# Out-projection of six feature blocks as fill of the scan's last chain, the first feed-forward pair in column halves, and an even spread of the modulation sums

## The chip, the cores and the metric

One core of a Trainium2 chip runs the whole kernel. The metric is the device time of one execution in microseconds, the median of several runs. TensorE (PE), VectorE (DVE), ScalarE (ACT), GpSimd (POOL) and SyncE (SP) each work through their own list of instructions in order; SP, and in places ACT and POOL, also issue the transfers (DMAs).

## What is computed

Two layers act on 512 tokens of 1,024 features, with 256 context tokens. The part that matters here is the first layer: an rwkv7 mixer (a scan in two directions over 16 heads), its out-projection, and a dense gated feed-forward.

```python
s_kk = einsum('bhvk,bhk->bhv', s, kk_t)          # one step of the scan
s = s * w_t - s_kk * (kk_t * a_t) + v_t * k_t
y_t = einsum('bhvk,bhk->bhv', s, r_t)
...
yn = ((y - mean) * rsqrt(var + 64e-5)) * lnx_g + lnx_b     # per head
mix = ((yn + coef * v) * gate) @ w_o                       # out-projection, 1024 x 1024
x = layer_norm(ALPHA * x + ada_gate * mix)                 # ALPHA = 4 ** 0.25
h = x * (1 + ada_scale) + ada_shift
x = layer_norm(ALPHA * x + ada_gate2 * ((silu(h @ w1) * (h @ w3)) @ w2))   # inner size 2816
```

The scales, shifts and gates ("modulations") are products of a conditioning vector with matrices of 1024 x 6144. Two more modulation vectors, called "1" and "2", are needed by the layers that follow.

## The kernel before

Every product of two float32 matrices is made from parts: each operand is split into a high part (an ACT cast to fp32r, `L167`) and a low part (a DVE subtraction, `L168`), and `mm3` issues three matmuls, high by high, high by low and low by high (`L173`).

**The scan** (`phase_rwkv`). The features are cut into 8 blocks f of 128. Each block has a chain of 12 steps; a step is a row of short dependent instructions: the ACT copy `Rs` (`L863`), PE matmuls (`L833`), the ACT copy `UV` (`L871`), PE again, and the DVE state update `S` (`L888`, `L890`). Between the links of the chain the program puts other work by `fill(n)`. It draws the next items of the generator `background()`, which holds the jobs of the next blocks' inputs (`job`, its matmuls are `L979`) and then the modulation items "0" (`ada`, matmuls `L235`). How many items are drawn by a slot is read from the table `PACE`; there are 384 slots, 48 to a chain. In `PACE` the last 40 items, all of them modulation items, lie evenly over the slots 268 to 384. The scan matmuls, the jobs and the modulation items share PE's one list. When a chain ends, `tail(f)` normalises its block on DVE, POOL and ACT, adds the bonus, gates it and stores the 128 x 512 block `yn` to `ygd` in DRAM.

**Out-projection and layer norm** (`L2112` to `L2134`). After the last tail the eight blocks are loaded into `xres`, split into the parts `y3`, and then `xres` is loaded anew with x. `w_o` comes as four loads of 1 MB and is split into 8 pairs of parts. For each block of 128 tokens (tb) PE does two halves of 24 matmuls of 128 x 512, `resid_add` adds gate times result (`L1314`, `L1318`), and `norm_tail` does the layer norm: statistics on DVE (`L1130`), the reciprocal root on POOL, the scaling on ACT (`L1139`), the affine part on POOL; at once eight PE transposes (`L1162`) and their splits give the columns of the features `hT`.

**Feed-forward** (`phase_ffn`). 22 inner blocks of 128 in three chunks of 8, 8 and 6. Each inner block (an `out`) takes 48 matmuls of 128 x 512 from `w1` and `w3`, then silu and a split; after each of the first two chunks `down` adds the chunk's product with `w2` (192 matmuls). All of `hT` has to be there before the first matmul. Beside it run the modulation sums (`ada_sum`), a generator `side` of 32 items: 12 groups for "1" and 12 for "2", with the sums of a group (PE, `L274`) three items behind it. A group is 8 loads of 256 KB into three buffers (`L283`) and 8 multiply-adds: on DVE for "1" (`L288`), on ACT and POOL for "2" (`L285`, `L286`). The loads of both are issued by SP, between those of the weights. In the program each `out` draws items: one at the first and two at the second of a pair for the first 16 blocks, then one each. The gates of the sums are read back by POOL (`L301`).

## Time and profile before

| | us |
|---|---|
| median of 3 runs (3021.52 to 3031.95) | 3023.82 |
| the profiled execution, its own time | 3030.04 |
| its span in the trace | 3028.3 |
| TensorE busy in the span | 2658.0 |
| VectorE busy | 1716.0 |
| ScalarE busy | 1333.8 |
| GpSimd busy | 825.0 |

The profiled execution is 6.2 us, or 0.2%, above the median. A busy share tells little by itself, since the stages have different limits; the rows below go by stage. A line of waits reads "engine, what it does, line <- who released it: us in total, times, longest". A line of the timeline gives start, duration, instruction, and in brackets the engine's idle time ahead of it with its releaser. Lines of `L...` are those of the kernel before.

### The profile page before, as it was taken

To read this page: it belongs to the slowest core of one execution; us is meant where nothing else is said; L and a number is where in the kernel's file an instruction comes from. 1 tells how busy PE (TensorE), PEld (TensorE's weight loads), DVE (VectorE), ACT (ScalarE), POOL (GpSimd) and SP (SyncE) were. 2 spreads that over 40 slices of the span, in tenths; PEclk is the share of its full clock that TensorE was granted. 3 is DMA by queue.
4 is the path that set the end of the run, shared out by engine and by line. 5 is a ranking of instruction groups with operands and counts; after the bars stand their busy time and mean duration, and the time that the engine had idled before them with its cause. 6 is when DMAs were issued, how large, how long until landed. Compare 5 with 4: busy or idle time off the path is not lost. (4 is left out here: it accounts for less than half of the span.)

```text
span 3028.3 us, 47973 instructions
## 1 busy us (share of the span) xinstructions
PE 2658.0 (88%) x18816; PEld 2001.1 (66%) x18816; DVE 1716.0 (57%) x2526; ACT 1333.8 (44%) x2338; POOL 825.0 (27%) x908
## 2 busy tenths in 40 slices
...
GB/s 257 182 222 66 96 125 142 181 137 129 172 133 95 186 129 165 222 189 212 186 150 63 306 258 271 258 258 287 233 239 88 68 43 74 56 84 94 102 90 64
DMA packets 301823, 477.92 MB, mean 158 GB/s; under 512 B 47282, under 2 KB 176067, under 8 KB 294935
## 3 DMA queue, kind: packets, MB, share of 16 engines
...
## 5 line engine op out<-in xcount | busy, mean ns | idle before, releaser
L168 DVE TENSOR_TENSOR wl<-w,wh 128x1024 fp32r<-128x1024 f32 (+2 forms) x400 | 477.3, 1203 | 622.3 <-ACT wh L167 618.9
L167 ACT CAST wh<-w 128x1024 fp32r<-128x1024 f32 (+2 forms) x400 | 382.8, 966 | 636.4 <-PE mm L173 438.8
L173 PE MATMUL mm<-act,wh 128*128 128x512 f32 x1408 | 441.1, 395 | 18.6 <-ACT act L167 14.8
L173 PEld LDWEIGHTS mm<-act,wh 128*128 128x128 f32 x1408 | 266.8, 190 | 78.7 <-ACT act L167 15.4
L173 PE MATMUL mm<-wh,act 128*128 128x512 f32 x948 | 308.1, 402 | 7.8 <-ACT wh L167 4.5
L173 PE MATMUL mm<-act,wl 128*128 128x512 f32 x704 | 277.3, 394 | 4.5 <-DVE wl L168 4.5
L173 PEld LDWEIGHTS mm<-wh,act 128*128 128x128 f32 x948 | 182.4, 194 | 57.3 <-issue 7.8
L173 PE MATMUL mm<-wl,act 128*128 128x512 f32 x474 | 190.9, 403 | 0.1
L286 POOL TENSOR_TENSOR act<-act 128x512 f32<-128x512 f32 x96 | 145.3, 1513 | 152.8 <-ACT act L285 137.8
L301 POOL DMA_DIRECT2D bc<-gate x6 | 3.6, 592 | 619.2 <-DVEq L1730 516.3
L173 PEld LDWEIGHTS mm<-act,wl 128*128 128x128 f32 x704 | 133.6, 190 | 36.3 <-DVE wl L168 8.4
L799 DVE STREAM_TRANSPOSE XT<-T 128x512 f16<-128x512 f16 x120 | 84.6, 705 | 99.8 <-ACT T L797 99.7
L743 POOL TENSOR_TENSOR GA<-GA,masks 128x512 f32<-128x512 f32 (+1 forms) x96 | 100.2, 1053 | 102.8 <-ACT GA L742 99.6
L285 ACT ACTIVATE act<-act,cT 128x512 f32<-128x512 f32 x96 | 68.4, 724 | 118.4 <-DMA act<-in_w_ada_dram 117.7
L739 PE MATMUL gm<-kr,bk 64*128 64x128 f32 (+1 forms) x768 | 115.7, 327 | 3.8 <-ACT GA L742 2.0
L792 DVE TENSOR_TENSOR W<-pW,masks 128x512 f16<-128x512 f32 x120 | 81.8, 681 | 63.5 <-PE pW L790 59.7
L739 PEld LDWEIGHTS gm<-kr,bk 64*128 64x128 f32 x768 | 99.7, 226 | 24.5 <-ACT GA L742 9.3
L173 PE MATMUL mm<-wh,moxl 128*128 128x512 f32 (+1 forms) x336 | 113.9, 382 | 0.0
L173 PEld LDWEIGHTS mm<-wl,act 128*128 128x128 f32 x474 | 91.8, 194 | 31.1 <-DVE wl L168 5.0
L850 POOL TENSOR_TENSOR SP<-S,pc 128x64 f32<-128x64 f32 x176 | 58.3, 349 | 196.2 <-DVE S L890 184.8
L173 PE MATMUL mm<-wh,moxh 128*128 128x512 f32 (+1 forms) x336 | 107.3, 389 | 4.9 <-ACT wh L167 4.9
L797 ACT CAST T<-pT 128x512 f16<-128x512 f32 x120 | 69.6, 580 | 84.1 <-PE pT L795 80.9
...
## 6 DMA issues: line engine op xcount, KB each, us to landing
w<-in_moe_w_dram SPq DMA_DIRECT2D x136, 512.0 KB
w<-in_moe_w_dram SPq DMA_DIRECT2D x40, 1024.0 KB
w<-in_ffn_w_dram SPq DMA_DIRECT2D x32, 1024.0 KB
...
w<-in_w_up_dram SPq DMA_DIRECT2D x22, 1024.0 KB
x<-xdk POOLq DMA_DIRECT2D x18, 1024.0 KB, 5.7
```

The source lines that it names most:

```text
L167: self.nc.scalar.copy(out=hi, in_=x)
L168: self.nc.vector.tensor_tensor(out=lo, in0=x, in1=hi.bitcast(F32), op=OP.subtract)
L173: self.nc.tensor.matmul(ps, x, y, start=start and i == 0, stop=stop and i == 2, skip_group_check=True)
L285: nc.scalar.activation(out=wt, in_=wt, func=AF.Copy, scale=c)
L286: nc.gpsimd.tensor_tensor(out=acc, in0=wt, in1=acc if kk else bias, op=OP.add)
L301: (eng or self.nc.gpsimd).dma_start(out=t, in_=row_ap.to_broadcast([128, D]))
L739: nc.tensor.matmul(pss[par][:, s2, d, :nc_], bkj(d, par, j), KR[d][PR(par), j::12, :][:, :nc_ // 64, :], start=True, stop=True)
L743: nc.gpsimd.tensor_tensor(out=out, in0=out, in1=gm, op=OP.mult)
L792: nc.vector.tensor_tensor(out=W16, in0=pW, in1=lmask[:, li, None].to_broadcast(sh), op=OP.mult)
L797: nc.scalar.copy(out=T16, in_=pT)
L799: nc.vector.transpose(fl(XT), fl(T16))
L850: nc.gpsimd.tensor_tensor(out=SP[:, d], in0=S[:, d], in1=PC[d][:, j:j + 1].to_broadcast([128, 64]), op=OP.mult)
```

## The change

1. `PACE`: the 40 modulation items now end at slot 322, and 50 draws follow up to slot 384, the end of the last chain. They are four jobs "o", one for each 256 output features: the product of feature blocks 0 to 5 with `w_o`, 72 matmuls of 128 x 256 in each (288 in all). Each loads `w_o` twice by SP, and x three times (1 MB each) by POOL's queue. Its result is gated, added to ALPHA x on DVE and stored to `ysums`.
2. `tail` splits `yn` into its two parts itself and stores them to `yparts`, in place of the store to `ygd`. In the last tail three operations go from POOL to DVE.
3. After the scan only blocks 6 and 7 are projected: 12 matmuls for each tb, where there were 48. Their parts come in two loads of 512 KB by POOL's queue, `xres` is loaded from `ysums`, and `w_o` in one load of 1 MB. The transposes of a tb (`turn`) are put behind the norm of the next one.
4. The first `out` does its columns 0 to 255 first, then `turn(3)`, then columns 256 to 511.
5. The loads of "1" and all bias loads go from SP's queue to POOL's. An item of `side` now follows each `out` and, in the first two chunks, each pair of additions of `down`; it is tied by `issue_after` to the instructions just ahead of it.

```diff
-        (220, 137), (236, 153), (252, 161), (268, 177), (384, 217))
+        (220, 137), (236, 153), (252, 161), (268, 177), (322, 217), (384, 267))
...
-            nc.sync.dma_start(out=bias[0:1], in_=b[None, c0:c0 + n])
+            nc.gpsimd.dma_start(out=bias[0:1], in_=b[None, c0:c0 + n])
             for kk in range(8):
                 wt, c = ws[kk % 3], self.cT[:, kk, row:row + 1]
-                nc.sync.dma_start(out=wt, in_=w[kk * 128:(kk + 1) * 128, c0:c0 + n])
+                (nc.sync if on_pool else nc.gpsimd).dma_start(out=wt, in_=w[kk * 128:(kk + 1) * 128, c0:c0 + n])
...
+    def o_out(p, pss, lat, pool, tag, *_):
+        g = k.t(pool, [128, 512], tag=tag)[:, :256]
+        nc.sync.dma_start(out=g, in_=k.gates["0"][0][:, p * 256:(p + 1) * 256].to_broadcast([128, 256]))
+        for i, ps in enumerate(pss):
+            t = k.t(pool, [128, 512], tag=tag)
+            rows = lambda x: x[i * 256:(i + 1) * 256, p * 256:(p + 1) * 256].rearrange("(b p) n -> p b n", p=128)
+            nc.sync.dma_start(out=halves(t), in_=rows(a["x"][0]))
+            nc.vector.tensor_tensor(out=halves(ps), in0=halves(ps), in1=g[:, None, :].to_broadcast([128, 2, 256]), op=OP.mult)
+            nc.vector.scalar_tensor_tensor(out=t, in0=t, scalar=ALPHA, in1=ps, op0=OP.mult, op1=OP.add)
+            nc.sync.dma_start(out=rows(yo["sums"]), in_=halves(t))
+        return
+    OUT = {"k": k_out, "r": r_out, "v": v_out, "o": o_out}
...
+            eng = nc.gpsimd if f < 7 else nc.vector
...
-            nc.sync.dma_start(out=yg[f], in_=yn)
+            hi, lo = (k.t(bst, [128, 512], F32R, tag="st") for _ in range(2))
+            k.part_to(hi, lo, yn)
+            for i, x in enumerate((hi, lo)):
+                nc.sync.dma_start(out=yo["parts"][:, f, i], in_=x.bitcast(F32))
+            made["y", f] = True
...
+            byrow, last_ = n_ in "vo", (6 if n_ == "o" else KB) - 1
...
+            for kk in range(last_ + 1):
...
+            for p in range(4):
+                assert all(made.get(("y", f)) for f in range(6))
+                yield from job("o", p, True)
...
-def norm_tail(k, sp, psp, tb, xres, gbc, bbc, hT, scol, bcol):
+def norm_rows(k, sp, tb, xres, gbc, bbc):
...
-    if hT is not None:
-        to_feature(k, sp, psp, xh, hT, slice(tb * 128, (tb + 1) * 128), scol, bcol)
+    return xh
...
+        if cols is not None and i == 0:
+            ws = [k.part(w[:, :, :128]) for w in (w1, w3)]
+            pss = [k.t(psp, [128, 512], tag="mm") for _ in ws]
+            for cs, make in cols:
+                make()
+                for w, ps in zip(ws, pss):
+                    for kk in range(KB):
+                        k.mm3(ps[:, cs], at(w, ALL, kk), at(xT, ALL, kk, cs), kk == 0 and cs.start == 0, kk == KB - 1 and cs.stop == n)
+        for w in (w1, w3) if not pss else ():
...
+    done = [0]
+    def tick(n, *behind):
+        with ExitStack() as es:
+            for x in behind:
+                es.enter_context(tc.issue_after(x.ins))
+            for _ in range(n):
+                done[0] += 1
+                if done[0] % 2 == 0:
+                    next(side, None)
...
-                k.part_to(*g[f - f0 + i], s)
-                for _ in range(1 + i if f < 16 else 1):
-                    next(side, None)
+                hi, lo = k.part_to(*g[f - f0 + i], s)
+                tick(2, hi, lo)
...
+        def add(tb, hf, ps):
+            x = resid_add(k, sp, tb, hf, ps, gate2, xres, ALPHA if f0 == 0 else None)
+            if f0 < 16:
+                tick(1, x)
...
-            with tc.tile_pool(reuse_waits="tile", name="wo3", bufs=5) as wo3:
-                y3 = feat()
-                yg = xres.rearrange("p t d -> p (t d)").rearrange("p (f n) -> p f n", f=KB)
-                for f in range(KB):
-                    nc.sync.dma_start(out=yg[:, f, :], in_=ygd[f])
-                for f in range(KB):
-                    k.part_to(*at(y3, ALL, f), yg[:, f, :])
-                nc.sync.dma_start(out=xres, in_=a["x"][0].rearrange("(t p) d -> p t d", p=128))
-                ws = []
-                for i in range(4):
-                    raw = k.load_w(a["rk_w_o"][0][(i % 2) * 512:(i % 2 + 1) * 512, (i // 2) * 512:(i // 2 + 1) * 512])
-                    ws += [k.part(raw[:, 2 * q:2 * q + 2, :], wo3 if len(ws) + q < 5 else k.wq) for q in range(2)]
-                hT = None
-                for tb in range(4):
-                    for hf in range(2):
-                        ps = k.t(psp, [128, 512], tag="mm")
-                        for kk in range(KB):
-                            k.mm3(ps, at(y3, ALL, kk, slice(tb * 128, (tb + 1) * 128)), at(ws[hf * 4 + kk // 2], ALL, kk % 2), kk == 0, kk == KB - 1)
-                        resid_add(k, sp, tb, hf, ps, gate, xres)
-                    hT = hT or feat()
-                    norm_tail(k, sp, psp, tb, xres, *gb, hT, *cols)
+            raw = k.load_w(a["rk_w_o"][0][768:1024, :])
+            ws = [k.part(raw[:, :, hf * 512:(hf + 1) * 512]) for hf in range(2)]
+            y67 = k.t(act, [128, 2, 2, NT], F32R, tag="act")
+            for i in range(2):
+                nc.gpsimd.dma_start(out=y67[:, i], in_=yo["parts"][:, 6 + i])
+            nc.sync.dma_start(out=xres, in_=yo["sums"].rearrange("(t p) d -> p t d", p=128))
+            hT = feat()
+            rows_ = {}
+            def norm(tb):
+                cs = slice(tb * 128, (tb + 1) * 128)
+                for hf in range(2):
+                    ps = k.t(psp, [128, 512], tag="mm")
+                    for i in range(2):
+                        k.mm3(ps, at((y67[:, i, 0], y67[:, i, 1]), ALL, cs), at(ws[hf], ALL, i), i == 0, i == 1)
+                    resid_add(k, sp, tb, hf, ps, gate, xres, None)
+                rows_[tb] = norm_rows(k, sp, tb, xres, *gb)
+            def turn(tb):
+                to_feature(k, sp, psp, rows_[tb], hT, slice(tb * 128, (tb + 1) * 128), *cols)
+            for tb in range(4):
+                norm(tb)
+                if tb:
+                    turn(tb - 1)
+            turns = [(slice(0, 256), lambda: None), (slice(256, 512), lambda: turn(3))]
```

ACT at the end of the scan, last steps of the last chain, before: `Rs` and `UV` belong to the chain, `wh<-w` is the high part of a weight, here always of `w_o` for the stage behind the scan.

```order
L871 ACTIVATE UV_12696<-ch_13601 64x128 x2
L167 CAST wh_13828<-w_13822 128x1024
L167 CAST wh_13834<-w_13832 128x1024
L167 CAST wh_13838<-w_13832 128x1024
L863 COPY Rs_13659<-ch_13646 128x128
L167 CAST wh_13804<-w_13802 128x1024
L167 CAST wh_13808<-w_13802 128x1024
L167 CAST wh_13814<-w_13812 128x1024
L167 CAST wh_13818<-w_13812 128x1024
L167 CAST wh_13824<-w_13822 128x1024
L871 ACTIVATE UV_12696<-ch_13646 64x128 x2
```

The same place after.

```order
L167 CAST wh_14034<-w_14032 128x512
L167 CAST wh_14247<-w_14245 128x1024
L167 CAST wh_14251<-w_14245 128x1024
L877 COPY Rs_14001<-ch_13988 128x128
L885 ACTIVATE UV_12952<-ch_13988 64x128 x2
L167 CAST wh_14494<-w_14490 128x1024
L877 COPY Rs_14062<-ch_14049 128x128
L885 ACTIVATE UV_12952<-ch_14049 64x128 x2
L877 COPY Rs_14115<-ch_14102 128x128
L1373 DMA plb<-in_cpool_dram 128x512
L1375 DMA plw<-in_pool_w_dram 128x8x256
L885 ACTIVATE UV_12952<-ch_14102 64x128 x2
```

Eight casts of `w_o` stood about the last `Rs`; now a cast of an "o" job and two of `w_o` stand ahead of the third last `Rs`, one of the feed-forward's `w1` (`w_14490`) behind the next `UV`, and none between the last two `UV`.

SP from the end of the last tail on, before: `ygd` holds the blocks, `in_ada_w` is the matrix of "1".

```order
L2118 DMA xres<-ygd 128x512 x2
L945 DMA ygd<-yn_13680 128x512
L2118 DMA xres<-ygd 128x512 x6
L2121 DMA xres<-in_x_dram 128x4x1024
L283 DMA act_14236<-in_ada_w_dram 128x512 x3
L280 DMA act_14236<-in_ada_b_dram 1x512
L155 DMA w_14625<-in_ffn_w_dram 128x8x256
L283 DMA act_14236<-in_ada_w_dram 128x512
```

The same place after: `st` are tiles of the "o" jobs and the parts of `yn`, `ysums` and `yparts` the new DRAM tensors.

```order
L371 DMA st_14117<-gate_221 128x256
L155 DMA w_14731<-in_ffn_w_dram 128x8x256
L375 DMA st_14119<-in_x_dram 128x2x256
L375 DMA st_14124<-in_x_dram 128x2x256
L378 DMA ysums<-st_14119 128x2x256
L378 DMA ysums<-st_14124 128x2x256
L963 DMA yparts<-st_14181 128x512
L2164 DMA xres<-ysums 128x4x1024
L963 DMA yparts<-st_14182 128x512
L155 DMA w_14899<-in_ffn_w_dram 128x8x256
```

The load of `xres` stood behind the loads of `ygd`; now it stands behind the last stores of `ysums` and the store of the first part of the last `yn`. The loads of `in_ada_w` have left this engine.

POOL from the end of the layer norm on, before: `bc<-gate` reads a gate of the sums back, `L286` adds up "2".

```order
L1148 TENSOR_TENSOR xres<-rsq_14185,bg_13763 128x1024
L1149 TENSOR_TENSOR xres<-xres,bb_13765 128x1024
L301 DMA bg_16922<-in_ln_g_dram 128x1024
L301 DMA bb_16924<-in_ln_b_dram 128x1024
L301 DMA bc_16917<-gate_14310 128x1024
L286 TENSOR_TENSOR act_14236<-act_14236 128x512 x16
L301 DMA bc_17521<-gate_14311 128x1024
L286 TENSOR_TENSOR act_14236<-act_14236 128x512 x80
```

The same engine in the feed-forward after, from the read of the first gate on.

```order
L301 DMA bc_17237<-gate_14630 128x1024
L283 DMA act_14484<-in_ada_w_dram 128x512 x8
L280 DMA act_14484<-in_ada_b_dram 1x16x32
L283 DMA act_14484<-in_ada_w_dram 128x512 x8
L280 DMA act_14484<-in_ada_b_dram 1x16x32
L283 DMA act_14484<-in_ada_w_dram 128x512 x8
L280 DMA act_14484<-in_ada_b_dram 1x16x32
L283 DMA act_14484<-in_ada_w_dram 128x512 x8
L280 DMA act_14484<-in_b_ada_dram 1x16x32
L283 DMA act_14484<-in_ada_w_dram 128x512 x4
L301 DMA bc_17841<-gate_14631 128x1024
L286 TENSOR_TENSOR act_14484<-act_14484 128x512 x2
```

The loads of "1" now stand on POOL, the last of them behind the read of the first gate of "1" (`gate_14630`), and the first addition of "2" behind the read of the second (`gate_14631`).

## Rows read from the trace of the kernel before

**Rows 1.** Page, its first line.

```profile
span 3028.3 us, 47973 instructions
```

**Rows 2.** Windows: length, busy us of PE, PEld, DVE, ACT, POOL; PEclk, DMA share, GB/s.

```profile
993.30:1052.80 59.50, 48.68 (x926) 33.45 (x927) 30.43 (x65) 26.43 (x69) 22.73 (x49) 0.88 0.59 188
1052.80:1067.00 14.20, 1.44 (x24) 1.06 (x20) 7.70 (x8) 8.47 (x11) 0.00 (x0) 0.50 0.48 165
1067.00:1081.40 14.40, 5.85 (x22) 3.01 (x21) 4.65 (x8) 3.45 (x7) 4.92 (x5) 0.50 0.96 305
...
1100.90:1180.00 79.10, 43.30 (x176) 35.44 (x176) 38.33 (x66) 18.81 (x31) 26.44 (x24) 0.76 0.25 79
...
1195.40:1280.00 84.60, 84.44 (x386) 68.40 (x384) 54.93 (x76) 21.77 (x29) 0.53 (x1) 1.00 0.71 231
1280.00:1305.00 25.00, 4.32 (x18) 4.17 (x19) 17.68 (x28) 3.61 (x5) 0.00 (x0) 0.59 0.52 167
...
1345.00:1577.00 232.00, 223.37 (x985) 177.20 (x983) 111.77 (x103) 121.71 (x169) 145.83 (x97) 0.99 0.60 191
```

**Rows 3.** Waits of PE from 1052 to 1182 us.

```profile
PE mm L1162 <- ACT rsq L1139: 31.3, 4, 12.1
...
PE ch L833 <- ACT Rs L863: 8.4, 1, 8.4
```

**Rows 4.** Timeline of ACT, the last chain's end.

```profile
1059.53 1.99 ACT L167 CAST wh<-w 128x1024 fp32r<-128x1024 f32 x2 [3.71 <-DMA w<-in_rk_w_o_dram]
```

**Rows 5.** Windows of the job matmuls (L979) alone, last thirds of two chains: PE, PEld.

```profile
757.30:795.90 38.60, 14.05 (x57) 8.36 (x57) 1.00 0.56 178
...
967.30:993.30 26.00, 0.00 (x0) 0.00 (x0) 1.00 0.33 95
```

**Rows 6.** Timeline of PE, a run of job matmuls.

```profile
803.12 0.28 PE L979 MATMUL bg<-wl,x 128*128 128x256 f32 x1
...
803.24 0.39 PE L979 MATMUL bg<-wh,x 128*128 128x256 f32 x2
...
803.59 0.28 PE L979 MATMUL bg<-wh,x 128*128 128x256 f32 x1
```

**Rows 7.** Windows of the modulation matmuls (L235) alone, last chain: PE, PEld.

```profile
993.30:1052.80 59.50, 9.79 (x104) 2.25 (x104) 0.88 0.59 188
```

**Rows 8.** Timeline, from the last block's store to the first residual sum.

```profile
1085.15 1.29 DVE L168 TENSOR_TENSOR act<-xres,act 128x512 fp32r<-128x512 f32 x2 [3.78 <-DMA ygd<-yn]
...
1091.65 0.38 SPq L2121 DMA_DIRECT2D xres<-in_x_dram  x1
...
1100.92 0.69 DVE L1318 SCALAR_TENSOR_TENSOR xres<-xres,silu 128x512 f32<-128x512 f32 x1 [4.99 <-DMA xres<-in_x_dram]
```

**Rows 9.** Groups of DVE by line, 1095 to 1184 us: busy us, mean ns.

```profile
L288 DVE SCALAR_TENSOR_TENSOR act<-act,cT 128x512 f32<-128x512 f32 x9 | 8.0, 890 | 3.0 <-DMA act<-in_ada_w_dram 2.6 <-DMA act<-in_ada_b_dram 0.3
```

**Rows 10.** Waits from 1180 to 1600 us.

```profile
POOL bc L301 <- DMA gate<-silu: 98.9, 2, 97.9
...
DVE act L288 <- DMA act<-in_ada_w_dram: 51.6, 37, 4.6
...
PE mm L274 <- DVE act L288: 20.8, 2, 11.4
```

**Rows 11.** Windows of the sums of "1" (L288) on DVE: busy us.

```profile
1164.00:1195.40 31.40, 14.05 (x18) 0.60 0.68 216
1195.40:1280.00 84.60, 34.50 (x46) 1.00 0.71 231
```

**Rows 12.** Window of the sums of "2" (L286) on POOL: busy us.

```profile
1465.00:1574.00 109.00, 72.09 (x48) 0.98 0.59 188
```

**Rows 13.** Page, DMA issues by POOL's queue: count, KB each, median us to landing.

```profile
x<-xdk POOLq DMA_DIRECT2D x18, 1024.0 KB, 5.7
...
bc<-gate POOLq DMA_DIRECT2D x6, 512.0 KB, 4.6
...
bb<-in_ln_b_dram POOLq DMA_DIRECT2D x2, 512.0 KB, 6.9
```

48 lines of the change are left out of this document (23 added, 25 removed).

## The prediction

> **What bounds the kernel now.** I read the busy times by stage first, since the page's shares mix stages with different limits. The profiled execution spans 3028.3 us [rows 1] and took 3030.04 us; the median is 3023.82. I sum differences on stages of the profiled execution and put them on the median; the 0.2% between the two would move a difference of 25 us by 0.05 us.
>
> Four stretches matter [rows 2]. The last chain of the scan (993.3 to 1052.8, 59.5 us) has PE busy for 48.7 us, so PE is nearly full but not quite. The next 14.2 us hold the chain's last links with PE busy for 1.4 us: PE waited 8.4 us in one piece for the last `Rs` [rows 3], which stood on ACT behind casts of `w_o` whose loads had not landed [rows 4]. From the chain's end at 1067.0 to the end of the first `out` at 1195.4, 128.4 us, no engine is full: the tail takes 14.4 us, and in the 79.1 us of norm PE is busy 43.3 and DVE 38.3 us [rows 2]. PE waits there in four pieces, 31.3 us in all, for the scaled rows of the norm [rows 3]: matmuls, residual and norm of one tb follow each other. That is latency, and the place where the change can gain. The feed-forward (1195.4 to 1577.0, 381.6 us) is bound by PE, which is busy 84.4 of the first 84.6 us, but for one hole of 25.0 us with 4.3 us of PE [rows 2]. PE waits there for the sums of "1" on DVE, 20.8 us [rows 10]. I call it a hole of 20.7 us, so PE alone needs some 361 us there.
>
> **Out-projection and norm: -54 us.** The tail's 14.4 us [rows 2] I leave as they are; the three operations that go from POOL to DVE should save about a microsecond. `yn` then goes through DRAM in two parts: the way of the old one, store and reload, cost DVE 3.8 us of waiting [rows 8]. The load of `xres` now stands on SP behind that store and the last stores of `ysums`. Before it was issued at 1091.65 and its first user ran at 1100.92 [rows 8], 9.3 us; the same length gives 14.4 + 3.8 + 9.3 = 27.5 us after the chain's end for the first residual sum. This is the new late one: 2 MB by one load, with nothing but the loads of blocks 6 and 7 beside it. The first tb's 12 matmuls, at the 0.25 us of this stretch (43.30 / 176, clock 0.76 [rows 2]), add 3.0 us if the load does not hide them. Then DVE sets the pace, as 12 matmuls of a tb (3 us) are shorter than its part of the norm: of its 38.3 us, 8.0 are sums of "1" [rows 2, 9], which no longer stand there, so 30.3 us for four tb. The first column half of the first `out` lies beside this, the second cannot: 48 matmuls of 256 columns at 0.12 us (next paragraph) are 5.8 us at full clock, 11.5 us at the half clock that the stretches at the chain's end show [rows 2]; I take the half clock, and 2 us for the silu. Sum: 27.5 + 3.0 + 30.3 + 11.5 + 2 = 74 us in place of 128.4. The bounds: with the second half at full clock and the first matmuls hidden 65; if the old stretch stays and loses only its 144 matmuls (79.1 - 36.0 = 43.1 in place of 30.3), 87. So -63 to -41.
>
> **The scan: +22 us.** The "o" jobs bring 288 matmuls. In a run of job matmuls four were issued between 803.12 and 803.59 [rows 6], 0.12 us each: 34.6 us of PE. The modulation items cost the same PE time, only earlier: 104 of their matmuls, 9.8 us busy, leave the last chain [rows 7] for the two before. About four fifths of the new draws fall in the last chain, whose PE had 59.5 - 48.7 = 10.8 us free [rows 2]; I let four fifths of that hide work: 34.6 - 8.6 = 26 us. The splits of the jobs (ACT and DVE, under half busy there) I cost at nothing because of that room; without it, they would hold up `Rs` and `UV`. The wait of 8.4 us at the last `Rs` should halve, not go: two casts of `w_o` and one of `w1` still stand ahead of late links on ACT, on loads that SP issues among the stores of the jobs. Net 26 - 4 = 22. Lower bound: the wait goes whole, and the clock, 0.88 in the last chain [rows 2] and 1.00 in stretches with jobs [rows 5], returns 12% of 48.7, 6 us: 12. Upper bound: the last third of a chain took 38.6 us with 57 job matmuls and 26.0 with none [rows 5], 0.22 us for each, 64 us for 288; but those thirds hold other parts of the next block's input too, so I stay near the PE time.
>
> **The feed-forward: +8 us.** Two rows of work run side by side here: PE with 361 us, and the sums. "1" took 84.6 / 46 = 1.84 us an operation [rows 11], "2" 109 / 48 = 2.27 [rows 12], each 96 times: 177 + 218 = 395 us. Before, they began at 1164, 31.4 us before the first `out` ended, with 18 operations done by then [rows 11], and so just fitted. Now an item is tied to the instructions ahead of it, and the first begins behind the first `out`. The loads of "1" come by POOL's queue, where none of 256 KB is in this trace. 1 MB lands in 5.7 us and 512 KB in 4.6 [rows 13]; drawn on, that is an estimate of 4.1 for 256 KB. With 0.6 us for the issue (my allowance) and 0.89 for the sum [rows 9], and three buffers, an operation costs 5.6 / 3 = 1.86 us, as before. POOL also reads the first gate of "1" back ahead of the last loads: it waited 97.9 us for such a gate [rows 10] where nothing was queued behind it; now the loads of the last groups of "1" are, and the first sum of "2" stands behind the second gate. So the sums would end 396 us or more after the first `out`, 14 over today. Against that, the even spread fills the hole of 20.7 us, and part of the 2.27 of "2" was waiting for its draws and for ACT: at 2.0 us the sums end at 370. I take the middle, 390, +8. Bounds: PE alone, 361, -20; the load at the 6.9 us of the slowest 512 KB row [rows 13], (6.9 + 1.5) / 3 = 2.8 us and 269 + 218 = 487, +105.
>
> Sum: -54 + 22 + 8 = -24, so 3000 us.
>
> **A rule for and a rule against.** The trace shows POOL's queue at 4.6 to 6.9 us for 512 KB [rows 13] with no row of 256 KB. The Trainium skill, "DMA: Bandwidth & Descriptors", section "Anatomy of one DMA — SWDGE (gpsimd) path", gives such a load 2.0 us and the bytes over 436 per ns, 2.6 us for 256 KB by that; the rows lie above its 3.2 for 512 KB. By it an operation of "1" would cost some 1.4 us, and the feed-forward would be bound by PE, which is the first rival. Against: "SBUF — State Buffer" of the Trainium skill, section "SBUF: two separate sides", warns that a load issued from GpSimd gets its descriptors written by that engine, which some VectorE operations lock out, and advises the ACT or SP queue. By it the loads of "1" would be slowest beside DVE's sums; that is the third rival. No row here shows either.
>
> **Rivals.** *The sums fall behind PE again.* For it: PE is busy 223.4 of 232.0 us in the last stretch with "2" beside it [rows 2], and the hole came only where groups of "1" were drawn too fast. Against: the late start. Feed-forward -20: 3024 - 54 + 22 - 20 = 2972.
> *The fill lies wholly on the chain's path.* PE takes its list in order, so each draw stands ahead of a link. At the 0.22 us of rows 5: 64 - 4 = 60 us, 3024 - 54 + 60 + 8 = 3038, slower. It decides from (46 + 4) / 288 = 0.17 us a matmul on; against it is that 0.12 is all the PE time of one and that the last chain prepares no next block.
> *The loads by POOL's queue hold "1" up.* At a landing of 6.9 us the feed-forward gains 105 us, 3024 - 54 + 22 + 105 = 3097. The change loses from 414 us of sums on, which is 2.04 us an operation and a landing of 4.6 us. That is the 512 KB row itself, so this is not far off; for it speak also that DVE is busy 54.9 of 84.6 us there [rows 2], against it that the load is half as large.
> *The norm stays latency-bound* at its upper bound: -41 in place of -54, 3013. It lies at the edge of my forecast.
>
> **Chances.** Forecast with its own range of 2985 to 3014: 0.52. First rival 0.18, second 0.12, third 0.13, the fourth or a mixture that ends within 0.3% 0.05. A measurement of this kernel tells no less than about 0.3%, 9 us, from no change. Faster: 0.52 less a little, and 0.18, 0.67. Same: the edge of the forecast, mild forms of the second and third, 0.18. Slower: 0.15. For 8 in 10 the range leaves out the strong form of the third rival and the best tenth: 2960 to 3038.
>
> **What would show it.** Chain end to first `out` near 74 us, with the first residual sum about 27 us in; if that sum comes after 32 us, the `xres` load is the step I had wrong. The last chain's 59.5 us at about 75 and the one before some 8 longer; a wait on `Rs` behind a cast of 4 us. From the first `out` to the last about 390 us, PE waiting for the sums of "1" in pieces under 10 us, and for "2" at the end. Loads of "1" spaced 1.85 us; over 2.04 the change loses its gain.

## The result: slower by 1.5%

The kernel after takes 3072.20 us (3064.14 to 3079.74), the kernel before, in the same comparison, 3025.38 us (3021.52 to 3031.95). The ratio is 1.0152, with a 95% interval of 1.0112 to 1.0192. The forecast was 3000 us, 0.8% faster, in a range of 2960 to 3038: wrong in sign and outside the range. The profiled execution of after took 3064.14 us; its span is 3062.4 us, 34.1 more than before [rows 1]. The medians lie 46.8 us apart, so the stages of the two profiled executions, compared below, show some 13 us less than the whole loss.

### The profile page after: what moved, and what is told of

The parts are those of the page before. It is cut to its first block, busy times and chain, and to the rows that moved or that the text cites. A ratio compares the mean times of both kernels' runs of the same rounds, so it can differ in the third digit from the quotient of the medians.

```text
span 3062.4 us, 48508 instructions
## 1 busy us (share of the span) xinstructions
PE 2665.4 (87%) x19008; PEld 2013.7 (66%) x19008; DVE 1729.1 (56%) x2551; ACT 1339.0 (44%) x2344; POOL 895.0 (29%) x1039
## 5 line engine op out<-in xcount | busy, mean ns | idle before, releaser
L173 PE MATMUL mm<-act,wh 128*128 128x512 f32 (+1 forms) x1440 | 446.5, 393 | 8.0 <-ACT act L167 8.0
L173 PEld LDWEIGHTS mm<-act,wh 128*128 128x128 f32 x1440 | 273.6, 193 | 68.3 <-ACT act L167 8.5
L173 PE MATMUL mm<-wh,act 128*128 128x512 f32 x852 | 276.5, 402 | 18.9 <-DMA act<-yparts 14.7
L173 PE MATMUL mm<-act,wl 128*128 128x512 f32 (+1 forms) x720 | 280.8, 390 | 0.0
L173 PEld LDWEIGHTS mm<-wh,act 128*128 128x128 f32 x852 | 163.6, 193 | 62.8 <-DMA act<-yparts 16.0
L173 PE MATMUL mm<-wl,act 128*128 128x512 f32 x426 | 170.9, 401 | 0.1
L286 POOL TENSOR_TENSOR act<-act 128x512 f32<-128x512 f32 x96 | 132.7, 1382 | 86.1 <-ACT act L285 83.2
L1000 PE MATMUL bg<-wh,x 128*128 128x256 f32 x480 | 126.2, 330 | 3.5 <-DMA x<-yparts 1.4
L864 POOL TENSOR_TENSOR SP<-S,pc 128x64 f32<-128x64 f32 x176 | 67.3, 400 | 189.3 <-DVE S L904 178.9
L288 DVE SCALAR_TENSOR_TENSOR act<-act,cT 128x512 f32<-128x512 f32 x96 | 72.0, 750 | 59.9 <-DMA act<-in_ada_w_dram 58.8
```

The lines of the kernel that those rows point to most:

```text
L173: self.nc.tensor.matmul(ps, x, y, start=start and i == 0, stop=stop and i == 2, skip_group_check=True)
L286: nc.gpsimd.tensor_tensor(out=acc, in0=wt, in1=acc if kk else bias, op=OP.add)
L288: nc.vector.scalar_tensor_tensor(out=acc, in0=wt, scalar=c, in1=acc if kk else bias, op0=OP.mult, op1=OP.add)
L864: nc.gpsimd.tensor_tensor(out=SP[:, d], in0=S[:, d], in1=PC[d][:, j:j + 1].to_broadcast([128, 64]), op=OP.mult)
L1000: m = nc.tensor.matmul(o, y, z, start=st and q == 0, stop=sp_ and q == 2, skip_group_check=True)
```

## The profile after

Windows of the kernel after, by stage (length; busy us of PE, PEld, DVE, ACT, POOL; granted clock, DMA share, GB/s), to be read beside [rows 2]: the scan in three pieces (chains f0 to f5, f6, f7), the way to the first residual sum, the norm to the silu of the first `out`, the first chunk with its `down` in two pieces, the second chunk's `out`s, the stretch from there to the last `out`, and what follows until the sums end.

```profile
205.00:910.50 705.50, 610.54 (x7948) 482.67 (x7946) 435.87 (x677) 374.12 (x822) 319.94 (x435) 0.84 0.44 138
910.50:1012.50 102.00, 94.03 (x1369) 69.55 (x1369) 62.56 (x105) 48.74 (x113) 45.12 (x65) 0.85 0.56 167
1012.50:1096.20 83.70, 67.72 (x1031) 57.17 (x1027) 45.00 (x81) 34.52 (x83) 24.22 (x48) 0.90 0.76 253
1096.20:1130.20 34.00, 16.31 (x66) 12.76 (x66) 9.03 (x15) 4.12 (x8) 3.89 (x5) 0.70 0.67 230
1130.20:1179.20 49.00, 26.93 (x157) 24.01 (x156) 34.02 (x57) 20.88 (x33) 28.61 (x28) 0.78 0.21 70
1179.20:1266.20 87.00, 87.00 (x399) 71.42 (x398) 58.95 (x80) 25.14 (x32) 25.66 (x48) 1.00 0.67 217
1266.20:1348.10 81.90, 64.31 (x258) 51.60 (x257) 55.09 (x80) 12.65 (x14) 24.91 (x47) 0.85 0.62 199
1348.10:1425.00 76.90, 76.90 (x342) 62.05 (x341) 40.11 (x47) 32.44 (x45) 27.90 (x30) 1.00 0.60 192
1425.00:1580.50 155.50, 129.23 (x540) 102.30 (x539) 55.13 (x56) 73.79 (x102) 96.96 (x77) 0.90 0.55 174
1580.50:1608.30 27.80, 1.91 (x2) 0.18 (x2) 8.80 (x8) 13.83 (x19) 19.48 (x15) 0.53 0.40 118
```

PE is full in the first and the second chunk, short of 17.6 us in the first `down`, of 26.3 us before the last `out`, and does almost nothing for 27.8 us behind it. The waits of PE from 1179 to 1700 us name the cause (who waits, for whom: us in total, times, longest):

```profile
PE mm L268 <- POOL act L286: 44.2, 4, 13.1
PE mm L274 <- DVE act L288: 17.6, 2, 10.6
PE mm L274 <- POOL act L286: 8.0, 3, 5.6
```

`L286` is the addition of "2" on POOL; `L268` and `L274` are the matmuls of the sums. In the program the last `down` is issued behind all items of `side`, so its matmuls stand behind the last sums in PE's list. In [rows 10] PE waited for "1" alone, 20.8 us; that hole is still there, 17.6 us, and a larger one for "2" is new. The last `L286` ended at 1608.3 us. Between the last sum of "1" and the first of "2" POOL stood still for the gate of "1" (its waits from 1360 to 1400 us):

```profile
POOL bc L301 <- DMA gate<-silu: 17.6, 1, 17.6
```

The table gives the stages of the profiled executions in us, each read from the timeline between two landmarks: the first `Rs` of a chain, the end of the last `UV`, the first residual sum, the start of the silu of the first `out` (with the load of its table), the ends of the products of `out` 9, 16 and 22, and the end of the span.

| stage | before | after | difference |
|---|---|---|---|
| up to the first `Rs` of the scan | 210.4 | 205.0 | -5.4 |
| chains f0 to f5 | 694.0 | 705.5 | +11.5 |
| chain f6 | 88.9 | 102.0 | +13.1 |
| chain f7 to its end | 73.7 | 83.7 | +10.0 |
| chain's end to the first residual sum | 33.9 | 34.0 | +0.1 |
| to the silu of the first `out` | 93.2 | 49.0 | -44.2 |
| to `out` 9 | 174.9 | 168.8 | -6.1 |
| to `out` 16 | 81.1 | 76.9 | -4.2 |
| to `out` 22 | 127.0 | 155.5 | +28.5 |
| behind `out` 22 | 1451.1 | 1481.9 | +30.8 |

Three sums matter: the scan +34.6, the out-projection and norm -44.1, the feed-forward and what waits behind it +49.0. The 5.4 us at the start lie ahead of the change. Later profiles of kernels with the old scan put its length, first `Rs` to chain's end, between 854 and 880 us where this profile has 857, so a single difference of 10 us in the scan tells little; chain f6 was 88.9 to 89.7 us in each of them.

## The experiments

Each was measured beside the kernel before, whose medians lay between 3024 and 3029 us there. "In the profile" means the one profiled execution.

### The queue or the draws

Run e1 puts the loads of "1" and the bias loads back on SP.

```diff
-            nc.gpsimd.dma_start(out=bias[0:1], ...)
+            nc.sync.dma_start(out=bias[0:1], ...)
-                (nc.sync if on_pool else nc.gpsimd).dma_start(out=wt, ...)
+                nc.sync.dma_start(out=wt, ...)
```

> The kernel after, with the loads of "1" and the bias loads back on SP's queue; draws and ties stay. Theory (the sums are drawn too late: the first begins behind the first out, the additions of "2" begin near out 14 and end after out 22, and everything behind waits for their end): "1" took 188.5 us for 96 operations, 1.96 us each, against 1.87 in the kernel before, so at most 10 us come back, 3055 to 3070 us. Rival (POOL's queue is what holds the sums up): the loss in and behind the feed-forward goes with it, about 40 us, 3030 us.

Measured: 3062.84 us, 1.0112 (1.0061 to 1.0163). About 10 us came back, though this interval and that of the kernel after overlap. "1" went from 188.5 to 172.0 us for its 96 operations. PE's waits from 1190 to 1700 us no longer name "1", but "2" as before:

```profile
PE mm L268 <- POOL act L286: 42.0, 4, 13.3
...
PE mm L274 <- POOL act L286: 7.5, 3, 6.1
```

From the silu of the first `out` to `out` 22 the profile has 383.7 us where after has 401.3 and before 383.1; behind `out` 22 it has 1481.8, as after. So POOL's queue is the smaller part, some 18 us in this stage, and with these draws the hole of 17.6 us for "1" is its work. Its loads of 256 KB landed in 3.2 us (median, issues of the kernel after), not in the 4.1 I had drawn on from larger ones:

```profile
act<-in_ada_w_dram POOLq DMA_DIRECT2D x96, 256.0 KB, 3.2
```

Run e2 keeps POOL's queue and takes back the draws.

```diff
-                tick(2, hi, lo)
+                for _ in range(1 + i if f < 16 else 1):
+                    next(side, None)
...
-            if f0 < 16:
-                tick(1, x)
```

> The kernel after with the draws of the kernel before (one and two per pair for the first 16 outs, then one, none in down, no tie to instructions ahead); the loads of "1" stay on POOL's queue. Theory (late draws): "2" begins by out 9 to 11 and is through by out 22, so 30 to 45 us come back, 3027 to 3042 us. Rival (POOL's queue): no more than 10 us come back, since "1" is as slow as with the new draws, 3062 us or more.

Measured: 3049.51 us, 1.0071 (1.0042 to 1.0099), 23 us under the kernel after. From `out` 16 to 22 it took 127.4 us and behind it 1452.9: both losses of the kernel after at the end were gone. Part was given back where the draws now came early: 58.2 us instead of 49.0 up to the first `out`, as sums of "1" stand in DVE's list there, and 114.2 instead of 86.9 us to `out` 8, where PE waits for them again. This run takes back the places of the draws and their ties to the `out`s together; which of the two counts was not tried.

Run e5 undoes both.

```diff
# the edits of e1 and of e2
```

> The kernel after with both undone: loads of "1" on SP's queue and the draws of the kernel before. What is left is the out-projection as fill, the new norm stage and the column halves. By the profiles of before and after the norm stage gave 44 us and the scan took 35: with the feed-forward as in the kernel before 3016 us. If the sums' chain stays the bound also with the old draws, because it starts no earlier than 80 us behind the scan's end, 3030 to 3045 us.

Measured: 3045.82 us, 1.0044 (1.0020 to 1.0069). The feed-forward and all behind it were as in the kernel before, so 17 us of loss were left in the scan and the out-projection, though I had expected a gain there. In the profile the scan took 902.5 us, 46 more than before, and the way from the chain's end to the silu 100.0, 27 less than before, where the kernel after has 44 less: the sums of "1" stand beside the norm again.

Run e10 is the reverse: the kernel before with the new draws alone.

```diff
-                for _ in range(1 + i if f < 16 else 1):
-                    next(side, None)
+                hi, lo = k.part_to(*g[f - f0 + i], s)
+                tick(2, hi, lo)
...
+            if f0 < 16:
+                tick(1, x)
```

> The kernel before with nothing but the new draws: one item behind each out, one behind each pair of additions in the first two downs, tied to the instructions ahead; loads on SP's queue, scan and out-projection as before. Theory (late draws): "2" begins near out 14, 14 of its additions are left at out 22, and 45 to 57 us are lost in the last outs and behind them, 3070 to 3085 us. Rival (the draws cost only together with the shorter norm stage or the POOL queue): 3020 to 3035 us.

Measured: 3053.12 us, 1.0099 (1.0077 to 1.0120): 28 us lost, less than the 45 to 57 expected. The profile has the 24 us before the last `out` and 27.5 behind it, as expected, and gains of 6 to 10 us in each of four earlier stages that I had not counted (the norm, the first chunk, its `down` and the second chunk, 31 us in all). PE's waits from 1190 to 1700 us, to be read as above:

```profile
PE mm L268 <- POOL act L286: 39.7, 4, 13.8
PE mm L274 <- POOL act L286: 6.7, 3, 5.5
```

So the draws alone bring the wait for "2", without the fill, the column halves and POOL's queue. They also fill the hole in the first `down`: no wait for "1" is left.

### The speed of the sums

Run e3 halves the sums: only four of the eight blocks of rows are added up.

```diff
-            for kk in range(8):
+            for kk in range(4):
```

> The kernel after, but the sums of "1" and "2" add up only four of their eight blocks of 128 rows, so half of their loads and additions are left out. Theory (the sums end last): PE no longer waits in or behind the feed-forward; the 17.6 us near the end of the first down, the 26.3 us before out 22 and the 26 us behind it go, 70 us, 2995 to 3005 us. Rival (the scan and the norm hold the loss, the sums are hidden): within 10 us of the kernel after, 3060 us.

Its total, 4871 us, can't be set beside the others: the router of the second layer sends its tokens by these modulations, and the part behind `out` 22 took 3345 us; what it would have taken against the 2995 to 3005 us expected is open. Up to there the profile can be read. From the silu of the first `out` to `out` 22 it took 337.4 us, 63.8 less than after (401.3), with no wait of PE for the sums. Windows of PE over this stage, before, after and e3 (length, busy us, clock):

```profile
1194.10:1577.10 383.00, 353.54 (x1558) 0.96 0.62 199
```

```profile
1179.20:1580.50 401.30, 357.44 (x1535) 0.93 0.60 192
```

```profile
1183.70:1521.20 337.50, 337.50 (x1523) 1.00 0.51 163
```

In e3 PE was busy throughout at full clock: 337 us is its own time here. In the kernel after it was idle for 43.9 us, and its busy time was 20 us longer, at a mean clock of 0.93.

Run e22 is the kernel after with one more load tile for the sums and one running sum less, in the same memory.

```diff
-        ... for o, m in ((0, 3), (3, 4), (7, 1)))
+        ... for o, m in ((0, 4), (4, 3), (7, 1)))
-            acc = accs[i % 4]
+            acc = accs[i % 3]
-                wt, c = ws[kk % 3], ...
+                wt, c = ws[kk % 4], ...
-            if len(pend) > 3:
+            if len(pend) > 2:
```

> The kernel after with four load tiles and three running sums, nothing else. "2" still begins near out 14; if the late start and not the speed is what costs, it gains little: 3050 to 3065 us. If the speed of the sums decides also here, 60 us less in the sums make 3015 to 3030 us.

Measured: 3012.49 us (2996.63 to 3026.59), 0.9960 (0.9932 to 0.9989) of the kernel before, and 60 us under the kernel after: the only version clearly under both. My own 3050 to 3065 was wrong, and the rival's 3015 to 3030 was near. The windows of the sums show why, "1" on DVE and "2" on POOL, first of the kernel after, from the first operation to the last:

```profile
1183.00:1372.30 189.30, 71.99 (x96) 0.94 0.66 214
```

```profile
1393.00:1608.30 215.30, 132.65 (x96) 0.87 0.54 168
```

Then of run e22:

```profile
1180.00:1335.00 155.00, 71.13 (x96) 0.98 0.75 249
```

```profile
1361.00:1538.50 177.50, 142.82 (x96) 0.93 0.67 214
```

From 1.96 to 1.61 us an operation for "1" (188.5 and 154.5 us of the windows), from 2.24 to 1.85 for "2". The work on DVE is the same, that on POOL 10 us more; what shrank is the waiting for loads, of "1" on DVE and of "2" on ACT, after and then in e22 (busy us, mean ns, idle time before and what ended it):

```profile
L288 DVE SCALAR_TENSOR_TENSOR act<-act,cT 128x512 f32<-128x512 f32 x96 | 72.0, 750 | 59.9 <-DMA act<-in_ada_w_dram 58.8
L285 ACT ACTIVATE act<-act,cT 128x512 f32<-128x512 f32 x96 | 68.1, 722 | 89.3 <-DMA act<-in_w_ada_dram 89.1
```

```profile
L288 DVE SCALAR_TENSOR_TENSOR act<-act,cT 128x512 f32<-128x512 f32 x96 | 71.3, 750 | 29.8 <-DMA act<-in_ada_w_dram 28.5
L285 ACT ACTIVATE act<-act,cT 128x512 f32<-128x512 f32 x96 | 67.2, 722 | 63.6 <-DMA act<-in_w_ada_dram 63.5
```

PE's waits in run e22, from 1140 to 1700 us:

```profile
PE mm L274 <- POOL act L286: 9.2, 5, 3.7
PE mm L268 <- POOL act L286: 5.9, 1, 5.9
...
PE mm L274 <- DVE act L288: 3.1, 1, 3.1
```

44.2 + 17.6 + 8.0 us had become 5.9 + 3.1 + 9.2. From the first `out` to the last it took 373.8 us, and 1445.0 behind it.

Run e21 does the same to the kernel before with column halves (run e9, below), run e20 to run e11 (below).

```diff
# the edit of e22
```

> Run e9 (the kernel before with the column halves) with four load tiles for the sums and three running sums, instead of three and four. Theory (the sums, 395 us in a row, bound the feed-forward of the kernel before: they end within 3 us of the last out, and waits for their loads, 52 us for "1" and 118 for "2", make up much of that): "1" goes from 1.87 to about 1.5 us an operation, "2" from 2.3 to about 1.9, the sums end 60 us or more earlier, PE's own 337 us from first to last out become the bound, and 20 to 45 us are won: 2980 to 3005 us. Rival (PE waits in its list for the place of the sums, not for their speed): 3015 to 3025 us.

Measured: 3027.04 us, 1.0005 (0.9983 to 1.0026): nothing won, against my expectation. The sums ended 27 us earlier in the profile (481.4 us behind the chain's end instead of 508.3), yet the `out`s came no sooner, 383.4 us from the first to the last. So with the old draws the length of the sums did not set the pace. PE still waited 16.5 us for "1" and 17.6 for "2"; the rival, that the places of the sums in PE's list count, fits this, but was not tried apart.

> Run e11 (the change with loads of "1" on SP, old draws, xres by ACT's queue) with four load tiles and three running sums. Theory as for run e21: from the first out to the last 345 to 360 us where run e11 has 381, 3005 to 3025 us in all, so the out-projection as fill stays behind run e21 by the 30 us that its scan costs, less the 30 that its norm stage gives. Rival: 3040 us.

Measured: 3034.41 us, 1.0027 (1.0008 to 1.0046), 381.8 us from first to last `out`: the same. So the new spread of the draws and faster sums need each other; either alone lost or won nothing. The two together on the kernel before, without the fill, were not run.

### The scan

Run e8 takes the fill out of the chains: the modulation items run to slot 384 as before, and the "o" jobs follow the last chain.

```diff
-        ... (268, 177), (322, 217), (384, 267))
+        ... (268, 177), (384, 217))
```

> The kernel after with the modulation items "0" spread to slot 384 as before; the four "o" jobs are run behind the last chain instead of in it. Tells what the fill costs the scan. In the kernel after, chains f0 to f5 together took 11 us more than before, f6 13 more, f7 to its end 10 more. Theory (the matmuls of the fill stand on the chain's path): f6 and f7 come back to 89 and 74 us, within 4; the 288 matmuls then take 35 us at full clock or 72 at half clock, behind the scan. Rival (the split and the two stores of each tail, or the clock, cost the chains their time): f6 and f7 stay 8 us or more above the kernel before. In both the chains f0 to f5 stay 10 us above it if the new tails are what slows them. Total 3065 to 3100 us.

Measured: 3145.03 us, 1.0414 (1.0391 to 1.0436). In the profile f6 took 112.1 us, f7 to its end 64.0, the scan 884.4. With no "o" matmul in the chains it was 28 us over the kernel before. The theory, by which f6 and f7 go back to 89 and 74 us, fell here. The jobs behind the scan brought the first residual sum to 109.9 us after the chain's end, 76 later, at a mean clock of 0.72; so the total lies above the 3065 to 3100 expected.

Run e12 is the kernel before with the split in the tails alone.

```diff
-            nc.sync.dma_start(out=yg[f], in_=yn)
+            hi, lo = (k.t(bst, [128, 512], F32R, tag="st") for _ in range(2))
+            k.part_to(hi, lo, yn)
+            for i, x in enumerate((hi, lo)):
+                nc.sync.dma_start(out=yg[:, f, i], in_=x.bitcast(F32))
...
-                    nc.sync.dma_start(out=yg[:, f, :], in_=ygd[f])
-                    k.part_to(*at(y3, ALL, f), yg[:, f, :])
+                        # four loads of the parts into y3 by POOL's queue
```

> The kernel before with the new end of the tail alone: each tail splits its block into two parts with two tiles of the jobs' output pool and stores both; the out-projection behind the scan loads the parts instead of splitting there. No fill is added. In run e8, which had no "o" matmul in the chains, the scan from its first Rs to its end took 884 us against 857 before and 891 in the kernel after. Theory (the split in the tails, 6 more instructions each on ACT and DVE and two tiles shared with the jobs, slows the chains, the fill hardly): 875 to 890 us from first Rs to chain end, 20 to 30 over the kernel before. Rival (the fill and the pulled-in modulation items are the cost, and run e8 paid for something else): 855 to 862 us. Total about 3024 plus that, less 5 to 10 for the splits that leave the out-projection stage.

Measured: 3073.99 us, 1.0124 (1.0078 to 1.0170): as much as the whole change, and above the expected 3034 to 3049. The scan took 907.5 us, f6 109.4, in a profile that lies 9 us above the median of its four executions.

Run e17 stores the block twice and splits nothing; run e18 is e12 with the high part made by DVE; run e13 is e11 with one shared tile for a split instead of two.

```diff
# e17
             nc.sync.dma_start(out=yg[f], in_=yn)
+            nc.sync.dma_start(out=yg[KB + f], in_=yn)
# e18
-            k.part_to(hi, lo, yn)
+            nc.vector.tensor_copy(hi, yn)
+            nc.vector.tensor_tensor(out=lo, in0=yn, in1=hi.bitcast(F32), op=OP.subtract)
# e13
-            hi, lo = (k.t(bst, [128, 512], F32R, tag="st") for _ in range(2))
+            hi, lo = k.t(bst, [128, 512], F32R, tag="st"), yn.bitcast(F32R)
```

> The kernel before with each tail's block stored twice to DRAM, no split: the second store of the new tail alone. If the store (SP's list, the DMA) slows the chains: 20 us or more over the kernel before, chain f6 over 100 us. If the split's instructions on ACT and DVE or the order that they bring do: no change, 3025 us, chain f6 at 89 us.

Measured: 3028.12 us, 1.0007 (0.9988 to 1.0026), f6 88.9 us. The store costs nothing.

> Run e12 (the kernel before with the split in the tails) with the high part made by DVE instead of ACT. If the cast in ACT's list, ahead of Rs and UV, holds the chains up: scan 20 us or more shorter than run e12's 908 us, total near 3045 us. If the work or the order counts, not the engine: within 10 us of run e12, 3070 us.

Measured: 3085.78 us, 1.0193 (1.0158 to 1.0227), scan 909.3 us. The cast's engine is not it.

> Run e11 with one tile of the shared pool for each split instead of two: the low part is written over yn. Theory (sharing two tiles with the jobs is what holds the chains up): the scan from first Rs to chain end falls from 895 us in run e11 by 10 to 25 us, and the total as much. Rival (the order of the instructions, or the work of the split itself): within 5 us of run e11, 3041 us.

Measured: 3053.35 us, 1.0070 (1.0047 to 1.0094), scan 918.2 us in the profile, 23 longer than in run e11 and not 10 to 25 shorter. The shared tile is not it either.

What then? A scheduler sets the order of the instructions, and two more in a tail change the places of very many others. Set side by side by the names of their tiles, up to the chain's end, ACT's 1172 and DVE's 997 instructions stand in the same order in before, e9, e15 and e17. In run e12 351 of ACT's, 247 of DVE's and 2584 of PE's 10833 stand elsewhere. So the second store of e17 cost nothing and moved nothing; the split moved a quarter of the list. Windows of PE over the scan show where the time is: length, busy us, clock. Before, e17, e15 (below, with nothing changed ahead of the out-projection), e8, e12, after and e16 (next), in this order:

```profile
210.40:1067.00 856.60, 737.21 (x10079) 0.83 0.43 131
```

```profile
201.30:1060.20 858.90, 739.67 (x10079) 0.83 0.44 135
```

```profile
206.60:1087.00 880.40, 765.01 (x10079) 0.80 0.41 128
```

```profile
211.90:1096.30 884.40, 757.95 (x10080) 0.81 0.43 133
```

```profile
203.30:1110.80 907.50, 770.40 (x10079) 0.79 0.42 127
```

```profile
205.00:1096.20 891.20, 772.29 (x10343) 0.85 0.49 152
```

```profile
205.10:1107.50 902.40, 786.54 (x10343) 0.83 0.45 138
```

Busy time times the clock is roughly PE's work at full clock. Over a whole scan that product is too coarse, since the mean clock counts idle time too; here it is summed over slices of 6 us of the same windows (to some 6 us):

| | work at full clock | lost to the clock | idle | scan |
|---|---|---|---|---|
| before | 621 | 116 | 119 | 857 |
| e17, second store | 619 | 120 | 119 | 859 |
| e15, the scan of before | 613 | 152 | 115 | 880 |
| e8, new tails, no fill | 618 | 140 | 126 | 884 |
| e12, split in the tails alone | 612 | 158 | 137 | 908 |
| after | 656 | 116 | 119 | 891 |
| e16, fill, old tails | 653 | 134 | 116 | 902 |

In e8 and e12 PE does the same matmuls as before, and most of the added time is a lower clock, the rest idle time. But e15 has the order of the kernel before and lost 36 us more to the clock, in a profile that lies 21 us above the median of its ten executions. So one profile does not show how much of the clock's part belongs to the split. The idle time does lie outside the 115 to 119 us of all profiles with the old order (126 in e8, 137 in e12, 139 in e18), and the medians of e12 and e18, 45 and 58 us over the kernel before, show a loss without the scan's profiles (of e12's, 9 us lie behind the scan in its profile). A place in chain f6 of run e12, slices of 6 us (length, PE busy, clock), and the pause in its second slice:

```profile
996.70:1002.70 6.00, 5.03 (x123) 1.00 0.52 160
1002.70:1008.70 6.00, 4.36 (x82) 0.84 0.52 150
1008.70:1014.70 6.00, 6.00 (x44) 0.50 0.01 3
1014.70:1020.70 6.00, 6.00 (x72) 0.50 0.15 31
1020.70:1026.70 6.00, 6.00 (x57) 0.50 0.16 61
1026.70:1032.70 6.00, 6.00 (x90) 0.67 0.22 52
```

```profile
1006.91 0.45 PE L790 MATMUL pW<-T,nl 128*128 128x64 f16 x5 [1.57 <-DVE T L783]
```

In the second slice PE was busy 4.36 of 6 us, with the pause of 1.57 us that ended at 1006.9; from then on it ran at half clock (1.2 of 2.4 GHz) for more than 18 us, busy all the time. In the kernel after the fill raises the work by 35 us, which is 288 matmuls at the 0.12 us of [rows 6], and both the idle time (119) and the loss to the clock (116) stay: the fill cost its own time; nothing of it hid, and nothing came back.

Run e16 keeps the fill, with the old tails; the "o" jobs split what they load.

```diff
-            hi, lo = (k.t(bst, [128, 512], F32R, tag="st") for _ in range(2))
-            k.part_to(hi, lo, yn)
...
+            nc.sync.dma_start(out=yo["parts"][:, f], in_=yn)
...
+                    if n_ == "o":
+                        nc.gpsimd.dma_start(out=x[:, :, 1], in_=xd[n_, n][:, kk:kk + nq])
+                        k.part_to(x[:, :, 0], x[:, :, 1], x[:, :, 1].bitcast(F32))
```

> Run e11 (loads of "1" on SP, old draws, xres by ACT's queue) with the tails of the kernel before: each stores its block whole, and the "o" jobs and the last stage split it when they load it (3 splits of 128 x 1024 in a job, 12 in all, where six tails had two of 128 x 512 each). The fill stays. Theory (the split in the tails is what slows the chains): chains f0 to f5 fall back to the kernel before, 694 us with a spread of 10; f6 and f7 to its end take 163 us plus the fill, 175 to 185; from the first Rs to the chain's end 870 to 880 us where run e11 has 895. Total 3010 to 3025 us. Rival (the fill): 890 us or more, total 3040 us.

Measured: 3038.70 us, 1.0034 (1.0016 to 1.0052). Chains f0 to f5 fell back to 699.1 us as expected, but f6 took 120.4 and f7 to its end 82.8, the scan 902: here the fill and its splits cost 40 us. So old tails with fill cost 46 us, new tails without fill 28 to 51, both together 35. These do not add up, and single profiles differ by some 25 us with the same order. That the order is what makes the pauses fits, but was not tried apart from the edits.

### The norm stage

Run e11 is e5 with the 2 MB load of `xres` issued by ACT's queue.

```diff
-            nc.sync.dma_start(out=xres, in_=yo["sums"]...)
+            nc.scalar.dma_start(out=xres, in_=yo["sums"]...)
```

> Run e5 (loads and draws as before) with one more change: the 2 MB load of xres is issued by ACT's queue, so that the store of the low part of the last block no longer stands behind it on SP. In the kernel after that store was issued at 17.7 us behind the chain's end and block 7's parts were loaded only from 26.3 on, the first residual sum came at 34 us. Expected: the load of block 7 begins 5 to 8 us earlier and the first residual sum too, 26 to 29 us; with the old draws the total follows by the same amount, some 6 us under run e5. If the load of block 7 waits for the transfer of xres itself (bandwidth), nothing moves.

Measured: 3041.01 us, 1.0067 (1.0030 to 1.0104), first residual sum 33.4 us behind the chain's end: nothing moved. The rows of the kernel after that led me there, on SP, POOL and PE (chain's end at 1096.2):

```profile
1113.28 0.55 SPq L2164 DMA_DIRECT2D xres<-ysums  x1
1113.91 0.51 SPq L963 DMA_DIRECT2D yparts<-st  x1
```

```profile
1122.50 0.53 POOL L2163 DMA_DIRECT2D act<-yparts  x1 [16.87 <-DMA yparts<-st]
```

```profile
1126.65 0.80 PE L173 MATMUL mm<-wh,act 128*128 128x512 f32 x1 [10.88 <-DMA act<-yparts]
```

The store of the low part was issued 0.6 us behind the load of `xres` and took 8 us to land; only then could POOL load block 7. In run e11 both stores were issued by 1124.8 and the load of block 7 still began 7.8 us later, with the 2 MB load of `xres` beside it. So the order on the queue is not the cause. The transfer of `xres` itself fits both runs, and run e16 bears it out: there the one store of block 7 was issued 3.2 us ahead of the load of `xres` and landed in 3.9 us, and then the load of block 7, beside `xres`, took 7.9 us from its issue for 256 KB. Rows of e16 on SP, POOL and ACT:

```profile
1121.72 0.33 SPq L960 DMA_DIRECT2D yparts<-yn  x1
```

```profile
1125.92 0.53 POOL L2163 DMA_DIRECT2D act<-yparts  x1 [7.82 <-DMA yparts<-yn]
```

```profile
1124.94 0.39 ACTq L2165 DMA_DIRECT2D xres<-ysums  x1
...
1133.80 0.62 ACT L167 CAST act<-act 128x512 fp32r<-128x512 f32 x1 [7.81 <-DMA act<-yparts]
```

The first residual sum came hardly sooner, 32.6 us behind the chain's end. A run without the 2 MB load was not made.

The stretch from the first residual sum to the silu, 49.0 us in the kernel after, is no row of DVE alone: DVE was busy 34.0 us of it and PE waited for scaled rows again. PE's waits from 1096.2 to 1179.2 us, and the first matmul of the second column half:

```profile
PE mm L1185 <- ACT rsq L1163: 19.9, 2, 14.3
```

```profile
1173.07 1.11 PE L173 MATMUL mm<-act,wh 128*128 128x256 f32 x4 [2.15 <-ACT act L167]
```

So the norm took 42.9 us up to the second half, and the second half 6.1 us, at full clock.

Run e9 is the kernel before with the column halves alone.

```diff
-                    norm_tail(k, sp, psp, tb, xres, *gb, hT, *cols)
+                    xh3 = norm_tail(k, sp, psp, tb, xres, *gb, hT if tb < 3 else None, *cols)
+            turns = [(slice(0, 256), lambda: None), (slice(256, 512), lambda: to_feature(k, sp, psp, xh3, ...))]
```

> The kernel before with the column halves alone: the first out does columns 0 to 255, then the transposes of the last tb, then the rest. The last of the four waits for scaled rows (31.3 us in all) is then covered by 48 half-width matmuls: the stretch from the chain's end to the first out gets 6 to 10 us shorter. If the feed-forward is bound by PE, 3018 us; if the sums are its bound as theory says of the kernel before (they end within 3 us of the last out), 3025 us, no change.

Measured: 3023.72 us, 1.0009 (0.9987 to 1.0031), 92.9 us in the norm where the kernel before had 93.2. The halves alone give nothing; the 6 to 10 us expected in the norm did not come.

### Two tries at a better draw

Runs e14 and e15 draw one item behind each of the first eight `out`s, four in each of the first two `down`s, three for each pair in the second chunk, untied, with "2" on DVE; e14 on run e13, e15 on run e9.

```diff
-                for _ in range(1 + i if f < 16 else 1):
+                for _ in range(1 + i if 8 <= f < 16 else 1):
...
+            if f0 < 16 and hf:
+                next(side, None)
...
-                    k.ada_sum(free, psp, sp, 2, ..., "2", True)
+                    k.ada_sum(free, psp, sp, 2, ..., "2", False)
```

> Run e13 with other draws and the sums of "2" on DVE like those of "1": one item behind each of the first eight outs, four in each of the first two downs, three behind each pair of the second chunk, nothing tied. An operation of "1" costs 1.84 us, one of "2" 2.27, so the sums need 41 us less and end before the last out. Expected from the first out to the last: 340 to 355 us where run e11 has 382, since with half the sums PE needed 337. Total 3000 to 3015 us. If DVE, waiting for loads in its own list, holds up the splits of the weights instead, no gain: 3040 us.

Measured: 3054.88 us, 1.0071 (1.0039 to 1.0102), 391.2 us from first to last `out`: no gain.

> The kernel before with the column halves, the same draws as run e14 and "2" on DVE; scan and out-projection as before. Theory as for run e14: 340 to 355 us from the first out to the last instead of 383, 2985 to 3000 us. Rival: DVE holds up PE, 3025 us or more.

Measured: 3029.39 us, 0.9999 (0.9977 to 1.0021), 392.5 us. In both the hole in the first `down` went (146 and 147 us to `out` 9 instead of 175), and the second chunk gave it back, 103 to 106 us instead of 81, with "2" in DVE's list among the splits of the weights. The rival of the expectation held.

## Why the forecast was wrong, step by step

**The stage behind the scan: right in kind, -44 for -54, and partly by luck.** The first residual sum came at 34.0 us, not 27.5. The step that failed there is the 3.8 us for store and reload of the last block: the low part took 8.1 us to land and block 7 another 4.1 to be loaded, and PE had to wait for it. The load of `xres`, which I had named as late, held nothing up as such; by runs e11 and e16 it is what the store landed beside. From there the stage took 49.0 us, where the terms of the forecast add up to 46.8, but two of them missed in opposite ways: the norm, with DVE to set the pace, was to take 33.3 us and took 42.9, close to the 43.1 of my upper bound, by which it stays bound by waits; and the second column half was to take 13.5 with its silu, at half clock, and took 6.1 up to the silu, at full clock.

**The scan: +34.6 for +22.** I let 8.6 us of the fill hide in PE's idle time; the idle time stayed at 119 us and the fill's 35 us of work came on top in full. That the wait at the last `Rs` halves came true, from 8.4 us in one piece [rows 3] to 4.6 in three, but did not shorten the whole. I did not price the tails' split at all; where it stands alone (runs e8 and e12) the scan took 28 and 51 us more, while in the kernel after no loss beyond the fill's own work is left to put down to it. The second rival, the fill wholly on the path, was right in kind and too dear at 0.22 us a matmul: +34.6 us over 288 is 0.12, the time of one matmul.

**The feed-forward: +49 for +8, the step that turned the sign.** The picture of two rows of work was right, the size of the second was not. I had the sums end at 396 us behind the first `out` and then took 390, on the hope that "2" would come down to 2.0 us; I called that the middle, but the middle of 396 and 370 is 383. Read from the profile: start 4.6, "1" 188.5, a gap of 21.4, "2" 214.6, together 429. "1" cost 1.96 us an operation, not 1.86, "2" 2.24, and the gap is what I had named without a price: POOL waited 17.6 us for the gate of "1" with "2" behind it. In the kernel before the same row reads start -30.0, "1" 180.0, gap 6.7, "2" 224.1, together 380.8. So the late start is the largest term, 34.6 of the 48.3 us by which the sums end later. And I ended the stage at the last `out`, while the sums ended 27.8 us behind it: of the 49 us, 30.8 lie where my sum had nothing. The end of the sums tells the loss of the whole stage and what stands behind it in every run with late sums: 48.3 us later and 49.0 lost in after, 30.8 and 31.4 in e1, 28.9 and 27.1 in e10, 17.2 and 19.0 in e2. Run e22 shows the term from the other side: 18.3 us earlier than before, 15.3 won, and 60 us under the kernel after in the medians, by faster sums alone.

**The third rival saw a part of the loss.** It gave POOL's queue as the cause. The 414 us of sums from which the change was to lose were passed, at 429, but by the late start and the gap: "1" stayed at 1.96 us an operation, under the 2.04 it named. The queue was worth some 10 us in the medians and 18 in the stage (run e1), not 105. The loads of 256 KB on it landed in 3.2 us, with DVE busy 59 of 87 us in the first chunk. The lock-out by some VectorE operations that the Trainium skill describes in "SBUF — State Buffer", section "SBUF: two separate sides", is not seen in these loads. The estimate of 2.6 us that the Trainium skill's rule in "DMA: Bandwidth & Descriptors", section "Anatomy of one DMA — SWDGE (gpsimd) path", gives is 0.6 us under the measured 3.2. The larger part was the later draws with their ties to the `out`s: runs e2 and e10.

**The first rival** did not come: PE waited for the sums. The floor of 361 us that it and I took was too high as well: PE's own time was 337 us (run e3), since the 361 held PE's waits beside the hole and busy time at a clock under 1.00. That the even spread fills the hole of 20.7 us came true in runs e1 and e10, with the loads on SP; on POOL's queue 17.6 us of waiting for "1" stayed.
